# S5's tables in two buffer sets with their parameters on GpSimd, and MoBA's bias rows in 32 pieces

## The chip, the cores and the metric

The kernel runs on one core of one Trainium2 chip. The metric is the time of the slowest core in device microseconds (us); lower is better. The engines are TensorE (PE in the profile), VectorE (DVE), ScalarE (ACT), GpSimd (POOL) and SyncE (SP), which here only issues DMAs. Each engine works through its own instructions strictly in the order in which the program was built, and waits on semaphores for the others.

## What is computed

A stack of four layers on 256 tokens of width 1024 in float32. A layer is an FFN, a mixer and an FFN again, each behind an RMS norm and added to the residual. The mixers are S5, HGRN2, a gated delta net and MoBA attention, in this order. The change touches the first FFN (beside which S5's parameters are prepared), S5, and the FFN behind S5 (beside which MoBA's rows of relative-position bias are written).

```python
def _swiglu(x, w_gate, w_up, w_down):
    return (jax.nn.silu(x @ w_gate) * (x @ w_up)) @ w_down

...

def _s5_mixer(u, lam_re, lam_im, log_dt, b_re, b_im, c_re, c_im, d_skip, w_glu):
    f32 = jnp.float32
    bsz, L, _ = u.shape
    lam = lax.complex(jnp.minimum(lam_re.astype(f32), -1e-4), lam_im.astype(f32))
    dt = jnp.exp(log_dt.astype(f32))[:, None]
    lam_bar = jnp.exp(lam * dt)
    b_bar = ((lam_bar - 1.0) / lam)[..., None] * lax.complex(b_re.astype(f32), b_im.astype(f32))
    ug = u.astype(f32).reshape(bsz, L, S5_GROUPS, S5_GROUP)
    bu = jnp.einsum('blgh,gph->lbgp', ug, b_bar)
    a = jnp.broadcast_to(lam_bar, (L, 1) + lam_bar.shape)

    def combine(e1, e2):
        a1, b1 = e1
        a2, b2 = e2
        return a1 * a2, a2 * b1 + b2

    _, h = lax.associative_scan(combine, (a, bu), axis=0)
    c = lax.complex(c_re.astype(f32), c_im.astype(f32))
    y = jnp.einsum('lbgp,ghp->blgh', h, c).real.reshape(bsz, L, D_MODEL)
    y = y + d_skip.astype(f32) * u.astype(f32)
    y = jax.nn.gelu(y).astype(u.dtype)
    val, gate = jnp.split(y @ w_glu, 2, axis=-1)
    return val * jax.nn.sigmoid(gate)
```

MoBA adds `table_t[:, _t5_bucket(qpos - kpos)]`, a bias by head and distance, to its attention logits.

## The kernel before

**Weights and steps.** All weights stream from HBM by DMAs on SP's queue (L69) into four raw buffers. ScalarE casts each unit of 128x1024 to `hi` (L86), VectorE subtracts to get `lo` (L87), and TensorE multiplies with both in three products (L343 to L345). There are four `hi` and four `lo` buffers, so a unit is cast at most four units ahead of its use. One unit, 12 matmuls of 512 columns, is a *step* of an FFN; the first FFN has 66, 44 for gate and up and 22 for down. After every four gate and up steps a column pair j is done: L423 (ScalarE, silu) and L426 (VectorE, gate times up) run once for each half of the tokens, and two to four steps later TensorE transposes the result (L435) and L438, L439 split it.

**Work beside the first FFN.** `step()` calls the generator `s5_prep` once or not at all per step (before: on odd steps from 5 to 31, then on every step up to 59):

```python
                if self.prep is not None and n > 4:
                    for _ in range(n % 2 if n < 32 else 1 if n < 60 else 0):
                        next(self.prep, None)
```

`s5_prep` loads S5's parameters, transposes lambda (`lam_in`, L606) and b and c (L621) on TensorE, and computes exp (`exp_m1`), sin and cos (`sin_cos_m1`), the powers `pw` of the transition (by `cmul`), its phase brought to length one (`unit`), and the factor for b (L671 to L682), all on tiles of 128x64 (`s5small`). For eight blocks j it then builds the tables: GpSimd makes the inward half (L728 to L730, twice three instructions of 128x512), VectorE the outward half (L733, L734, L736, 128x1024), both in one tile `s5e`. TensorE forms the token kernel from it (L742) and transposes the inward half (L756); the tables go to DRAM (`s_out`, `s_k`, `s_in`). Last, `s5_phases` computes the powers of the phase for the scan on GpSimd, for the first half of the groups.

**S5.** `load` in `s5` fetches the tables back from DRAM into five buffers (`tab`; inward, token and outward ones, each in four parts). The second half of the phases is computed on GpSimd once the FFN is done. `xr` (L939) and the half-turn `tb` (L894, beside VectorE's scan at L900) run on GpSimd as well; `busy` (L249) fills TensorE's time with matmuls without use.

**MoBA's bias rows.** `moba_bias` runs in the FFN behind S5: it spreads a table over 8 rows of 384 on GpSimd and writes `bias_rows` (8 x 128 x 384, 1536 KB) to DRAM with one DMA on ScalarE's queue (L1713).

**What sets the order.** The program is written in the order of the calls; a scheduler of the framework then moves instructions within each engine's order by what they depend on, except those that `keep_in_program_order` pins. Buffers come from pools: a tile with the tag of an earlier one waits until that one's last reader is done.

## Time and profile before

| what | us |
|---|---|
| median of 3 runs (2221.56 to 2225.37) | 2224.2 |
| the profiled execution | 2227.23 |
| its span | 2225.5 |
| first FFN, TensorE's first to last matmul | 9.9 to 243.7 |
| S5, up to its gated output's first matmul | 243.7 to 296.1 |
| GpSimd, table blocks j = 0 to 7 | 109.6 to 204.3 |
| GpSimd, phases, first half | 205.6 to 230.2 |
| bias rows, issue of the write | 348.7 |

The page of a profile gives busy times per engine and per group of instructions; a line number is that of the kernel. The window view gives the same for stretches of the span, with the granted TensorE clock (1.00 is full speed). The wait view names what an engine waited for last: `PE aux L756 <- POOL s5e L730` is TensorE at L756 waiting for GpSimd's write of `s5e` at L730. `SPq` and `ACTq` rows are the issues of DMAs on these queues; their duration is that of the issue, not of the transfer.

### The profile page before, as it was taken

How to read it: one execution, taken by the hardware profiler on the slowest of the kernel's cores; microseconds unless marked ns; L12 is line 12 of the kernel's file. 1: busy time of each engine (PE TensorE's matmuls, PEld its weight loads, DVE VectorE, ACT ScalarE, POOL GpSimd, SP SyncE). 2: the span in 40 equal slices, each digit the busy share in tenths (PEclk: the TensorE clock that was granted, in tenths of full speed). 3: DMA queues.
4: the chain of work that ended last, by engine and by line, in shares of the span. 5: the costliest groups of instructions: out<-in, count | busy, mean ns of one | idle time of the engine just before them, and what ended most of it. 6: DMA issues, size and time to landing. Idle time of an engine off the chain costs nothing.

```text
span 2225.5 us, 30259 instructions
## 1 busy us (share of the span) xinstructions
PE 2142.0 (96%) x11480; PEld 1768.3 (79%) x11480; DVE 1452.5 (65%) x2445; ACT 1159.0 (52%) x1876; POOL 207.8 (9%) x272
## 2 busy tenths in 40 slices
PE   8988888999999999999999999998999999999998
PEld 6766666888888888888788887787888888898886
DVE  7987674556555977555655788887555555666555
ACT  6434344445444855444544677764544544555443
POOL 0598600000000000001000000000000000000000
PEclk9999999999999999999999999999999999999999
DMA  8655966655555554655555543334555655655553
GB/s 252 191 193 200 250 184 161 205 175 191 186 189 190 171 168 136 189 178 189 176 180 176 163 141 105 105 115 131 175 186 180 199 182 187 199 162 170 189 180 105
DMA packets 317907, 389.64 MB, mean 175 GB/s; under 512 B 14192, under 2 KB 247856, under 8 KB 316736
## 3 DMA queue, kind: packets, MB, share of 16 engines
q1 hardware_dynamic: 314768, 383.92, 54.5%
q10 hardware_dynamic: 2800, 3.68, 0.9%
q8 instruction: 90, 1.47, 0.3%
q14 instruction: 57, 0.47, 0.1%
q0 software_dynamic: 192, 0.10, 0.0%
HBM read 375.65 MB, written 12.01 MB: 174 GB/s over the span
## 4 chain that ended last, share of the span: by engine, by line
PE 80%; ACT 5%; DVE 5%; issue 4%; DMA 3%; POOL 2%; SPq 0%; ACTq 0%; POOLq 0%; DVEq 0%
PE acc L343 23%; PE acc L345 23%; PE acc L344 23%; PE acc L311 2%; PE aux L435 2%; PE acc L312 2%; DVE lo L87 2%; PE acc L313 2%; ACT hi L86 1%; DMA raw<-in_ffn_w_up_dram 1%; ACT zb L1512 1%; PE aux L226 1%; POOL s5e L730 1%; POOL s5e L729 1%; POOL s5tmp L728 1%
## 5 line engine op out<-in xcount | busy, mean ns | idle before, releaser
L87 DVE TENSOR_TENSOR lo<-raw,hi 128x1024 fp32r<-128x1024 f32 x681 | 850.0, 1250 | 585.3 <-ACT hi L86 583.6
L86 ACT CAST hi<-raw 128x1024 fp32r<-128x1024 f32 x681 | 713.0, 1049 | 703.0 <-PE acc L345 648.0
L343 PE MATMUL acc<-hi,xhl 128*128 128x512 f32 x1568 | 625.7, 399 | 8.6 <-ACT hi L86 8.2
L344 PE MATMUL acc<-lo,xhl 128*128 128x512 f32 x1568 | 615.9, 393 | 2.4 <-DVE lo L87 2.3
L345 PE MATMUL acc<-hi,xhl 128*128 128x512 f32 x1568 | 615.3, 393 | 0.0
L343 PEld LDWEIGHTS acc<-hi,xhl 128*128 128x128 f32 x1568 | 296.1, 189 | 70.8 <-ACT hi L86 9.1
L345 PEld LDWEIGHTS acc<-hi,xhl 128*128 128x128 f32 x1568 | 296.0, 189 | 64.4 <-issue 0.9
L344 PEld LDWEIGHTS acc<-lo,xhl 128*128 128x128 f32 x1568 | 296.6, 189 | 63.6 <-DVE lo L87 5.1
L343 PE MATMUL acc<-hi,hhl 128*128 128x512 f32 x704 | 276.3, 392 | 0.0
L345 PE MATMUL acc<-hi,hhl 128*128 128x512 f32 x704 | 276.1, 392 | 0.0
L344 PE MATMUL acc<-lo,hhl 128*128 128x512 f32 x704 | 275.0, 391 | 0.0
L344 PEld LDWEIGHTS acc<-lo,hhl 128*128 128x128 f32 x704 | 132.5, 188 | 27.4
L345 PEld LDWEIGHTS acc<-hi,hhl 128*128 128x128 f32 x704 | 132.5, 188 | 27.4
L343 PEld LDWEIGHTS acc<-hi,hhl 128*128 128x128 f32 x704 | 132.6, 188 | 27.0
L313 PE MATMUL acc<-xhl,lo 128*128 128x256 f32 x520 | 150.0, 290 | 0.0
L311 PE MATMUL acc<-xhl,hi 128*128 128x256 f32 x520 | 149.7, 291 | 0.0
L312 PE MATMUL acc<-xhl,hi 128*128 128x256 f32 x520 | 148.4, 288 | 0.0
L423 ACT ACTIVATE sl<-acc,norm_r 128x256 f32<-128x256 f32 x176 | 83.6, 475 | 109.3 <-PE acc L345 88.6
L426 DVE TENSOR_TENSOR h<-acc,sl 128x256 f32<-128x256 f32 x176 | 74.0, 420 | 49.8 <-ACT sl L423 49.8
L313 PEld LDWEIGHTS acc<-xhl,lo 128*128 128x128 f32 x520 | 100.1, 193 | 2.0 <-DVE lo L87 1.0
L311 PEld LDWEIGHTS acc<-xhl,hi 128*128 128x128 f32 x520 | 99.7, 193 | 1.8 <-issue 0.9
L312 PEld LDWEIGHTS acc<-xhl,hi 128*128 128x128 f32 x520 | 99.9, 193 | 1.3 <-issue 1.1
(563 smaller groups left out, 2148.5 us busy)
## 6 DMA issues: line engine op xcount, KB each, us to landing
raw<-in_ffn_w_gate_dram SPq DMA_DIRECT2D x174, 512.0 KB, 3.8
raw<-in_ffn_w_up_dram SPq DMA_DIRECT2D x174, 512.0 KB, 4.8
raw<-in_ffn_w_down_dram SPq DMA_DIRECT2D x80, 1024.0 KB, 4.9
raw<-in_gdn_w_in_dram SPq DMA_DIRECT2D x24, 1024.0 KB, 5.2
raw<-in_hg_w_in_dram SPq DMA_DIRECT2D x16, 1024.0 KB, 5.4
raw<-in_moba_w_in_dram SPq DMA_DIRECT2D x12, 1024.0 KB, 5.1
raw<-in_ffn_w_down_dram SPq DMA_DIRECT2D x16, 512.0 KB, 3.7
raw<-in_s_w_glu_dram SPq DMA_DIRECT2D x16, 512.0 KB, 6.1
```

Of the source, the lines that this page charges most:

```text
L86: pin(self.nc.scalar.copy(hi, src))
L87: self.nc.vector.tensor_tensor(lo, src, hi.bitcast(F32), op=OP.subtract)
L226: nc.tensor.transpose(q[:, j * 128:j * 128 + 128], self.x[:, t, k * 128:k * 128 + 128], self.ident)
L311: t.matmul(p, hi, ah, start=first, stop=False)
L312: t.matmul(p, hi, al, start=False, stop=False)
L313: t.matmul(p, lo, ah, start=False, stop=last)
L343: mm(p, ah, hi[:, j], start=first and j == 0, stop=False)
L344: mm(p, ah, lo[:, j], start=False, stop=False)
L345: mm(p, al, hi[:, j], start=False, stop=last and j == n - 1)
L423: nc.scalar.activation(sl, p[:, :256], AF.Silu, scale=self.r_col[:, t:t + 1])
L426: return nc.vector.tensor_tensor(waiting[-1][1][:, t], p[:, 256:], sl, op=OP.mult)
L435: nc.tensor.transpose(q[:, c:c + 128], h[:, t, f * 128:f * 128 + 128], self.ident)
```

## The change

- `exp_m1`, `sin_cos_m1`, the powers and the phase unit run on GpSimd in place of VectorE. [...] The copies of the unit into `s5l` and of `pw` into `s5kk` go from GpSimd to ScalarE (L680 and L724 of the new kernel). The factor for b stays on VectorE (L686 to L697).
- The tables get a second set, `s5f` beside `s5e`; blocks j alternate. A block takes four calls of `s5_prep` in place of two, and its inward half is transposed one block later (`turned(j - 1)`). `step()` calls the generator at step 2, 6 to 18, and from 26 on.
- `s5_load` is taken out of `s5`, there are six `tab` buffers in place of five, and the first six loads (four inward, two token parts) are written in `s5_prep`, with one phase step behind each.
- The bias rows are written by 32 DMAs of 48 KB, one per step of the FFN.

```diff
             steps = [0]
+            bias = None
+            if self.prep is None and self.bias is not None:
+                bias = self.bias(pool)
+                self.bias = None
 
             def step():
                 steps[0] += 1
                 n = steps[0]
                 if n % 4 == 1 and waiting and n > 4:
                     turn()
-                if self.prep is not None and n > 4:
-                    for _ in range(n % 2 if n < 32 else 1 if n < 60 else 0):
-                        next(self.prep, None)
+                if bias is not None and n > 4:
+                    next(bias, None)
+
+                if self.prep is not None and (n == 2 or 5 < n < 19 or n > 25):
+                    next(self.prep, None)
...
+    def stt(self, eng, out, a, s, b, op0, op1, t=None):
+
+        t = out if t is None else t
+        eng.tensor_scalar(t, a, s, None, op0=op0)
+        eng.tensor_tensor(out, t, b, op=op1)
+
     def exp_m1(self, slots, x):
 
-        v = self.nc.vector
+        v = self.nc.gpsimd
...
-        v.scalar_tensor_tensor(r, n, -0.693359375, r, op0=OP.mult, op1=OP.add)
-        v.scalar_tensor_tensor(r, n, 2.12194440e-4, r, op0=OP.mult, op1=OP.add)
+        self.stt(v, r, n, -0.693359375, r, OP.mult, OP.add, t)
+        self.stt(v, r, n, 2.12194440e-4, r, OP.mult, OP.add, t)
...
+        g = nc.gpsimd
         _, dt = yield from self.exp_m1(slots, dt_in)
         yield
         ab = [slots.pop(), slots.pop()]
         for out, a in zip(ab, (lr, li)):
-            v.tensor_tensor(out, a, dt, op=OP.mult)
+            g.tensor_tensor(out, a, dt, op=OP.mult)
...
-        v.scalar_tensor_tensor(nr, cm, 1.0, em, op0=OP.add, op1=OP.mult)
-        v.tensor_tensor(nr, nr, cm, op=OP.add)
-        v.tensor_tensor(ni, ex, sn, op=OP.mult)
-        v.memset(pw[:, 0, :, 0], 1.0)
-        v.memset(pw[:, 1, :, 0], 0.0)
-        v.tensor_scalar(pw[:, 0, :, 1], nr, 1.0, None, op0=OP.add)
-        v.tensor_copy(pw[:, 1, :, 1], ni)
+        self.stt(g, nr, cm, 1.0, em, OP.add, OP.mult)
...
-                      [tmp[:, c, :64 * m].rearrange("p (g m) -> p g m", m=m) for c in range(2)])
+                      [tmp[:, c, :64 * m].rearrange("p (g m) -> p g m", m=m) for c in range(2)], g)
...
-        self.unit((cs, sn8), (tmp[:, 0, :64], tmp[:, 0, 64:128]), v)
+            g.tensor_tensor(tmp[:, 0, :64], cs, cs, op=OP.mult)
+            g.tensor_tensor(tmp[:, 0, 64:128], sn8, sn8, op=OP.mult)
+            self.stt(g, sn8, cs, 2.0, sn8, OP.mult, OP.mult, tmp[:, 0, 128:192])
+            g.tensor_tensor(cs, tmp[:, 0, :64], tmp[:, 0, 64:128], op=OP.subtract)
+            g.tensor_tensor(ex, ex, ex, op=OP.mult)
+        self.unit((cs, sn8), (tmp[:, 0, :64], tmp[:, 0, 64:128]), g)
         self.s5_l = pool.tile([128, 3, 32], F32, name="s5l")
-        for q in range(4):
+
+        def places(q):
             for a in range(2):
                 for n, t in enumerate((cs, sn8, ex)):
-                    nc.gpsimd.tensor_copy(self.s5_l[q * 32:q * 32 + 32, n].rearrange("p (j g a) -> p j g a", j=8, g=2)[:, :, :, a],
-                                          t[a * 32:a * 32 + 32].rearrange("p (j q g) -> p j q g", j=8, q=4)[:, :, q])
+                    nc.scalar.copy(self.s5_l[q * 32:q * 32 + 32, n].rearrange("p (j g a) -> p j g a", j=8, g=2)[:, :, :, a],
+                                   t[a * 32:a * 32 + 32].rearrange("p (j q g) -> p j q g", j=8, q=4)[:, :, q])
+
+        yield
...
+        places(0)
         yield
...
+        places(1)
...
+        places(2)
+        places(3)
...
-            nc.gpsimd.tensor_copy(back[:, :, :, n], pw[:, :, :, 8 - n])
+            nc.scalar.copy(back[:, :, :, n], pw[:, :, :, 8 - n])
         e = pool.tile([128, 16, 128], F32, name="s5e", tag="s5C")
-        eo, ebs = e[:, :8], (e[:, 8:12], e[:, 12:16])
+        more = pool.tile([128, 16, 128], F32, name="s5f", tag="s5G")
+        eos = e[:, :8], more[:, :8]
+        ebs = [(t[:, 8:12], t[:, 12:16]) for t in (e, more)]
...
+        def turned(j):
+
+            for n, eb in enumerate(ebs[j % 2]):
+                p = self.aux.tile([128, 512], F32, name="aux")
+                for g in range(4):
+                    nc.tensor.transpose(p[:, g * 128:g * 128 + 128], eb[:, g], self.ident)
+                nc.scalar.copy(et.rearrange("p g c -> p (g c)"), p)
+                dma(as_ap(self.s5_in, (8 * j + 4 * n) * 128, [[8192, 128], [128, 4], [1, 128]]), et)
+
         for j in range(8):
             r = slice(8 * j, 8 * j + 8)
-
-            rs = (slice(8 * j, 8 * j + 4), slice(8 * j + 4, 8 * j + 8))
-            for h, eb in zip(rs, ebs):
+            eo = eos[j % 2]
+
+            for n, eb in enumerate(ebs[j % 2]):
+                h = slice(8 * j + 4 * n, 8 * j + 4 * n + 4)
...
             dma(as_ap(self.s5_out, j * 1024, [[8192, 128], [128, 8], [1, 128]]), eo)
+            yield
...
+            if j:
+                turned(j - 1)
             yield
-            for h, eb in zip(rs, ebs):
-                p = self.aux.tile([128, 512], F32, name="aux")
-                for g in range(4):
-                    nc.tensor.transpose(p[:, g * 128:g * 128 + 128], eb[:, g], self.ident)
-                nc.scalar.copy(et.rearrange("p g c -> p (g c)"), p)
-                dma(as_ap(self.s5_in, h.start * 128, [[8192, 128], [128, 4], [1, 128]]), et)
-
+            yield
+        turned(7)
+
+        self.s5_tags = ["s5" + c for c in "ABCDEG"]
+        self.s5_tabs = []
         self.s5_turn = pool.tile([128, 2, 16, 32], F32, name="s5turn", tag="s5pw")
-        yield from self.s5_phases(self.s5_turn, 0, pool)
+        phases = self.s5_phases(self.s5_turn, 0, pool)
+        for kind, part in (("in", 0), ("in", 1), ("in", 2), ("in", 3), ("t", 0), ("t", 1)):
+            self.s5_tabs.append(self.s5_load(kind, part))
+            next(phases, None)
+            yield
...
+    def s5_load(self, kind, part):
+
+        tags = self.s5_tags
+        tags.append(tags.pop(0))
+        t = self.s5_pool.tile([128, 16, 128], F32, name="tab", tag=tags[-1])
+        if kind == "t":
+
+            for s in range(8):
+                self.nc.sync.dma_start(t[s * 16:s * 16 + 16],
+                                       as_ap(self.s5_k, part * 16 * 3840 + (7 - s) * 16, [[240, 16], [3840, 16], [1, 128]]))
+        else:
+            src = self.s5_in if kind == "in" else self.s5_out
+            self.nc.sync.dma_start(t, as_ap(src, part * 2048, [[8192, 128], [128, 16], [1, 128]]))
+        return t.rearrange("p (j q g) c -> p j q g c", q=4, g=2)
...
-        tags = ["s5" + c for c in "ABCDE"]
+        tags = self.s5_tags
...
+            if self.s5_tabs:
+                return self.s5_tabs.pop(0)
+            return self.s5_load(kind, part)
...
-        nc.scalar.dma_start(self.bias_rows, row.rearrange("h (o s) -> h o s", o=1).to_broadcast([8, 128, 384]))
+        for k in range(0, 128, 4):
+            yield
+            self.tc.keep_in_program_order(nc.scalar.dma_start(
+                as_ap(self.bias_rows, k * 384, [[128 * 384, 8], [384, 4], [1, 384]]),
+                row.rearrange("h (o s) -> h o s", o=1).to_broadcast([8, 4, 384])))
```

What the change moves on VectorE, in the first FFN around the second column pair (L87 is a weight's `lo`, L426 gate times up, L439 the split). Before, the rows from the tenth L87 on:

```order
L87 TENSOR_TENSOR lo<-raw,hi 128x1024 x2
L426 TENSOR_TENSOR h<-acc,sl 128x256 x2
L87 TENSOR_TENSOR lo<-raw,hi 128x1024
L607 TENSOR_SCALAR s5small<-aux 128x64
L608 COPY s5small<-aux 128x64
```

The changed kernel, from the eleventh L87 on:

```order
L87 TENSOR_TENSOR lo<-raw,hi 128x1024
L426 TENSOR_TENSOR h<-acc,sl 128x256
L691 TENSOR_TENSOR s5small<-s5small 128x64
L426 TENSOR_TENSOR h<-acc,sl 128x256
L690 TENSOR_TENSOR s5small<-s5small 128x64
L692 TENSOR_TENSOR s5small<-s5small 128x64
L695 TENSOR_TENSOR s5small<-s5small 128x64
```

L691 and L690 multiply with the transition minus one, which GpSimd now makes (L655 and L654), and they stand around the second L426 of the pair.

On ScalarE of the changed kernel, the rows from the thirteenth cast on (L680 copies the unit, L423 is the silu, L438 the split's cast); before, no copy of this kind stood on ScalarE:

```order
L86 CAST hi<-raw 128x1024 x2
L680 COPY s5l<-s5small 32x16 x3
L86 CAST hi<-raw 128x1024
L680 COPY s5l<-s5small 32x16 x4
L423 ACTIVATE sl<-acc,norm_r 128x256
L680 COPY s5l<-s5small 32x16 x9
L86 CAST hi<-raw 128x1024
L423 ACTIVATE sl<-acc,norm_r 128x256
L680 COPY s5l<-s5small 32x16 x8
```

The copies, which need the end of GpSimd's unit, now stand ahead of cast 15 and of the third pair's L423.

On SP's queue at the end of the first FFN (`s_in`, `s_out` and `s_k` are the tables in DRAM, `tab` their buffers for S5, `w_glu` S5's output weights), before:

```order
L758 DMA s_in<-s5tmp 128x512
L69 DMA raw<-in_ffn_w_down_dram 128x2x512
L69 DMA raw<-in_s_w_glu_dram 128x4x256 x2
L804 DMA tab<-s_in 128x2048
L69 DMA raw<-in_s_w_glu_dram 128x4x256 x2
L804 DMA tab<-s_in 128x2048
L69 DMA raw<-in_s_w_glu_dram 128x4x256 x4
L804 DMA tab<-s_in 128x2048 x2
L800 DMA tab<-s_k 16x16x128 x16
L804 DMA tab<-s_out 128x2048 x2
```

and in the changed kernel:

```order
L748 DMA s_in<-s5tmp 128x512
L829 DMA tab<-s_in 128x2048
L748 DMA s_in<-s5tmp 128x512
L69 DMA raw<-in_s_w_glu_dram 128x4x256 x2
L748 DMA s_in<-s5tmp 128x512
L69 DMA raw<-in_s_w_glu_dram 128x4x256 x2
L829 DMA tab<-s_in 128x2048 x3
L825 DMA tab<-s_k 16x16x128 x13
L829 DMA tab<-s_out 128x2048 x2
```

The last writes of the inward table now lie between the loads of S5's output weights, and three inward tables and 13 pieces of the token tables behind them; three pieces stand earlier, between the last weights of the FFN.

More of the change, by code (lines that the diff above doesn't have):

```diff
@@ L455, in ffn @@
             nc.vector.tensor_scalar(half, self.r_col, 0.5, None, op0=OP.mult)
-            if self.prep is None and self.bias is not None:
-                self.bias(pool)
-                self.bias = None
             ahead = self.ahead
@@ L540, in sin_cos_m1 @@
     def sin_cos_m1(self, slots, x):
-        v = self.nc.vector
-        t, n, r, z, s, c, a, b, k, odd = [slots.pop() for _ in range(10)]
-        k, odd = k.bitcast(I32), odd.bitcast(I32)
+        v = self.nc.gpsimd
+        t, n, r, z, s, c, a, b = [slots.pop() for _ in range(8)]
         big = 12582912.0
```

58 lines of the change are left out of this document (25 added, 33 removed).

## The prediction

> **What bounds the kernel now.** The page comes first: the busy time of each engine over the whole span.
>
> ```profile
> PE 2142.0 (96%) x11480; PEld 1768.3 (79%) x11480; DVE 1452.5 (65%) x2445; ACT 1159.0 (52%) x1876; POOL 207.8 (9%) x272
> ```
>
> TensorE is busy for 96% of the span, so an edit off TensorE can only win where TensorE stands still or runs at a lowered clock. The change touches the first FFN (to about 244 us), S5 behind it (to about 296) and the FFN after that. Second, the windows over the stretches in question (columns: from:to, us, busy time and instructions of PE, PEld, DVE, ACT and POOL, the granted PE clock, DMA share, GB/s):
>
> ```profile
> 10.00:100.00 90.00, 87.39 (x396) 69.57 (x397) 82.69 (x225) 54.04 (x81) 19.09 (x26) 1.00 0.71 218
> 100.00:240.00 140.00, 122.53 (x664) 97.10 (x663) 104.22 (x78) 57.98 (x89) 117.37 (x109) 0.96 0.64 218
> 140.00:150.00 10.00, 5.22 (x21) 3.90 (x20) 9.90 (x7) 2.84 (x5) 9.76 (x6) 0.70 0.56 198
> 370.00:390.00 20.00, 12.70 (x45) 9.58 (x44) 5.08 (x7) 5.30 (x7) 0.00 (x0) 0.74 0.79 210
> ```
>
> Up to 100 us TensorE loses 2.6 of 90 us: **there it is the bound, and what is put in its way costs in full**. From 100 to 240 it is idle for 17.5 us, and the clock of 0.96 costs 4% of 122.5, 4.9 more: 22.4 us are to be won. The row of 140 to 150 shows what a stall leaves behind: 5.22 busy us at 0.70 lose another 1.6. Around 380 us stands a third loss.
>
> Third, TensorE's waits up to 330 us, by what ended them (total, times, longest):
>
> ```profile
> PE acc L878 <- DMA tab<-s_k: 11.9, 3, 5.0
> PE aux L756 <- POOL s5e L730: 11.2, 5, 3.5
> PE aux L742 <- DVE s5e L736: 6.2, 3, 3.2
> ```
>
> L756 and L742 work on S5's tables within the first FFN, and POOL and DVE deliver these too late; L878 is S5 itself.
>
> **The change part by part. GpSimd's chain.** exp, sin and cos, the powers and the phase unit leave DVE for GpSimd. DVE's pace in that chain, and GpSimd's with the same shape in the phases, from the timeline (start, us):
>
> ```profile
> 47.15 0.22 DVE L526 TENSOR_TENSOR s5small<-s5small 128x64 f32<-128x64 f32 x1
> 47.41 0.20 DVE L527 TENSOR_SCALAR s5small<-s5small 128x64 f32<-128x64 f32 x1
> 47.64 0.23 DVE L528 TENSOR_TENSOR s5small<-s5small 128x64 f32<-128x64 f32 x1
> ```
>
> ```profile
> 212.47 0.31 POOL L495 TENSOR_TENSOR s5t<-s5turn 128x64 f32<-128x64 f32 x1
> 212.74 0.31 POOL L496 TENSOR_TENSOR s5t<-s5turn 128x64 f32<-128x64 f32 x1
> 213.13 0.32 POOL L497 TENSOR_TENSOR s5turn<-s5t 128x64 f32<-128x64 f32 x1
> 213.53 1.20 POOL L498 TENSOR_TENSOR s5t<-s5turn 128x64 f32<-128x64 f32 x1
> ```
>
> DVE does two dependent instructions in 0.49 us, 0.245 each. On GpSimd an independent one follows after 0.27, a dependent one after 0.39, and one that meets a two-input DVE instruction takes 0.9 longer (1.20 for 0.31). One-input instructions of this shape are not in the trace. The ends are 0.27 (nothing depends) and 0.42 (all depend, some meet DVE); I take **0.35**, nearer the upper one, since most of the chain depends and half of it has one input.
>
> The Trainium skill ("GPSIMD Engine Reference", 4.1 Engine selection) calls GpSimd about two times slower than VectorE at two-input elementwise work and near line rate with one input. The rows give 0.31 to 0.22, or 1.4, at this size. By a factor of two the pitch would be 0.49, and the sum by it stands among the rivals.
>
> When does the chain start, and who waits for it? TensorE's and DVE's timelines around its start:
>
> ```profile
> 29.77 0.39 PE L343 MATMUL acc<-hi,xhl 128*128 128x512 f32 x1
> ...
> 32.95 0.39 PE L345 MATMUL acc<-hi,xhl 128*128 128x512 f32 x1
> ...
> 39.36 0.27 PE L606 MATMUL aux<-ident,lam_in 64*128 64x64 f32 x1
> ...
> 41.39 1.10 PE L621 MATMUL aux<-ident,s5b_in 64*128 64x64 f32 x8
> 42.42 0.66 PE L435 MATMUL aux<-ident,h 128*128 128x128 f32 x4
> ```
>
> ```profile
> 37.03 0.42 DVE L426 TENSOR_TENSOR h<-acc,sl 128x256 f32<-128x256 f32 x1 [0.94 <-ACT sl L423]
> 37.97 1.23 DVE L87 TENSOR_TENSOR lo<-raw,hi 128x1024 fp32r<-128x1024 f32 x1 [0.51 <-ACT hi L86]
> ```
>
> Places in TensorE's order are told in weight steps of 12 matmuls; from 29.77 to 32.95 the first and last of 15 stand, so one takes 0.227 and a step 2.73. Lambda's second transpose (39.36, step 9.08) moves to step 6.75, which is 39.36 - 2.33 x 2.73 = 33.0, and its copy ends at about 33.4. Then, in GpSimd's new order, 71 instructions end with L655: at 0.35 that is 58.3, with a meeting or so **59**. Up to the end of the powers stand 11 small ones and 18 of 64 to 256 columns (0.36, 0.5 and 0.7 each, between the row of 64 and one of 512 below): **74** with a few meetings. The unit has 21 small ones (7.4), the 1024-column L703 stands among them (about 2), and meetings with DVE add some 3: **86**. So the chain is 52.6 us long, and 0.01 of pitch moves its end by 1.5.
>
> In DVE's new order L691, which reads L655's product, stands ahead of the second L426 of the column pair j = 1. That one ran at 37.03; now it runs at 59.5, and TensorE's transposes L435 wait for it at step 9.08. Undisturbed, TensorE would be there at 43 (39.4 and some 3.6 for the 32 transposes L632 that now stand ahead, at most 1.10 per eight). It starts at 60.5: **17 us** of waiting. Since weights are cast at most four steps ahead, nothing runs meanwhile. At about 86 the second wait ends: ScalarE's copies L680, which stand behind its cast 14 and read the unit. GpSimd's time for these is known:
>
> ```profile
> L667 POOL COPY s5l<-s5small 32x16 f32<-32x16 f32 x24 | 14.6, 609 | 66.1 <-DVE s5small L661 55.8 <-DVE s5small L510 9.4
> ```
>
> On ScalarE the trace has none; between 0 and 0.61 each I take 0.25. Sixteen of them stand ahead of the second L423 of j = 2, 4 us, and with two casts, L423 and L426 the product comes at 94.5. TensorE's transposes at step 13.08, due at 43 + 4 x 2.73 + 0.6 = 54.4, start at 94.8: **+40.4**, and with two restarts at 1.6 **+43.6**. A pitch of 0.27 makes it 32, 0.42 makes it 54.
>
> **Steps 31 to 61.** Two table sets, and four steps per j in place of two, take the waits of L742 and L756 away: **-22.4**. What is late next? GpSimd and DVE slow each other. First the two groups from 109.6 to 204.3 us (busy, mean ns), then each of the two operations in a moment with less company (the L87 at 37.97 above is alone):
>
> ```profile
> L730 POOL TENSOR_TENSOR s5e<-s5e,s5tmp 128x512 f32<-128x512 f32 x16 | 31.6, 1975 | 0.6
> ```
>
> ```profile
> L87 DVE TENSOR_TENSOR lo<-raw,hi 128x1024 fp32r<-128x1024 f32 x22 | 40.5, 1842 | 14.3 <-ACT hi L86 14.3
> ```
>
> ```profile
> 109.62 1.06 POOL L728 TENSOR_TENSOR s5tmp<-s5D,s5kk 128x512 f32<-128x512 f32 x1
> ```
>
> 1.06 becomes 1.98, and 1.23 becomes 1.84. In 94.7 us eight tables and 22 L87 were done: 11.8 us per j with 2.75 of them. With four it is 11.8 + 1.25 x 1.23 = 13.4. TensorE needs 4 x 2.73 and twelve transposes of 0.165 in four steps of gate and up, some 13.0, and with eight of them 12.2 in four of down. Of j = 2 to 7 most stand in the down part, and **+5** is left over: net **-17.4**.
>
> The Trainium skill ("SBUF — State Buffer", Who interferes with whom) has a two-input VectorE instruction and a GpSimd instruction that reads SBUF shut each other out for a whole instruction. The trace agrees nearly: by it a j of before is (2.75 + 2.5) x 1.23 + 6 x 1.06 = 12.8, and 11.8 was measured. By the rule a new j takes 15.0, which would leave 14 us in place of 5.
>
> **S5.** What ends it now, by the chain of waits; SP's issues of the table pieces; DVE's longest wait there; GpSimd's phases, first half 205.61 to 230.16, second from 243.99:
>
> ```profile
> 260.72 12.02 DMA tab<-s_out
> 272.75 6.30 DMA tab<-s_k
> ```
>
> ```profile
> 237.70 22.11 SPq L800 DMA_DIRECT2D tab<-s_k  x16
> ```
>
> ```profile
> DVE inc L900 <- POOL tb L894: 7.2, 1, 7.2
> ```
>
> ```profile
> 205.61 0.22 POOL L495 TENSOR_TENSOR s5t<-s5turn 128x16 f32<-128x16 f32 x1
> ...
> 229.73 0.43 POOL L500 TENSOR_TENSOR s5turn<-s5t 128x112 f32<-128x112 f32 x1
> 243.99 0.13 POOL L768 MEMSET turn<- 128x16 f32 x1 [13.83 <-PE acc L345]
> ```
>
> Six tables are asked for within the FFN, but on SP three inward ones and 13 of 16 pieces of the token tables stand behind the last write of the inward table, whose copy on ScalarE follows cast 66, so about 1 us ahead of the FFN's end. Then come the landing of that write, the three tables and 13 pieces at 1.38 (22.11 / 16), 18 us: done 20 us or so behind the FFN's end, where before it was 16 (259.8 against 244): **+3 on SP**. GpSimd gets later too: its last table waits for TensorE's step 55.25, some 33 us ahead of the end; 13.4 for the table and 24.5 for the first half end 5 us behind the FFN's end, and the second half, which started right at that end, starts 5 later. DVE waits for it already. The two lie beside each other, and with the little slack that GpSimd has I take **+4**; the ends are -4 (SP meets free buffers and shorter issues) and +6.
>
> **The bias rows.** TensorE's wait from 370 to 390 us, and the issues on ScalarE's and SP's queues ahead of it:
>
> ```profile
> PE acc L343 <- ACT hi L86: 6.8, 1, 6.8
> ```
>
> ```profile
> 348.66 0.79 ACTq L1713 DMA_DIRECT2D bias_rows<-row  x1
> ```
>
> ```profile
> 364.80 9.74 SPq L69 DMA_DIRECT2D raw<-in_ffn_w_up_dram  x1
> ```
>
> Behind one write of 1536 KB an issue of weights took 9.74 us, and TensorE ran 45 matmuls in 20 us where 88 fit. If 48 KB a step leave no hole, 43 x 0.227 = **-9.8**. The 32 issues at 0.79 are 25 us of ScalarE, hidden in its idle time (busy 54 of 90 us in the first FFN); without that cover one delays a cast by 0.8. The ends are 0 and -9.8; I take the gain.
>
> **Sum.** 43.6 - 17.4 + 4 - 9.8 = **+20.4** on the profiled execution's 2227.2 us (a span of 2225.5 and 1.7 around it): 2247.6. The median of the runs lies 3.0 lower, at 2224.2, so the forecast is **2244.6**.
>
> **Rivals.**
> - *GpSimd's small operations are quick* (the other side: faster). One-input instructions could need far less than 0.27, and the early wait shrinks by 1.5 per 0.01. This decides below a pitch of 0.21, where the sum is nothing; at 0.15 it is 20.4 - 30 = -9.6, or 2214.6. Without any early wait it would be 2201. Against it: 16 columns (205.61) still take 0.22.
> - *GpSimd at twice DVE's time*: a pitch of 0.49, +21, 2266. For it stands that all the chain depends; against it the 0.39 at 212.74.
> - *Full exclusion in steps 31 to 61*: +9, 2254. The 11.8 against 12.8 speaks against it.
> - *The bias pieces win nothing*, since all 1536 KB are still written: +9.8, 2254. Against it: 48 KB in 2.73 us are 18 GB/s beside some 210.
>
> **How the numbers follow.** The forecast gets 0.57 (2232 to 2256, by pitches of 0.27 to 0.42 and S5's ends), quick operations 0.16, twice DVE's time 0.07, full exclusion 0.10, the bias 0.10. The range leaves out the quicker half of the first rival and the slowest of the others: 2210 to 2264. A measurement of this kernel tells about 0.2%, 4.4 us, from no change. Faster by more than that: 0.16, the first rival. Within it: 0.09, the forecast's low end. Slower: 0.75.
>
> **What would show it.** Right: DVE's L691 and ScalarE's L680 wait for POOL; TensorE's waits name L435 <- DVE with some 17 us, and about 20 more before 100 us; L774 and L746, the new lines of L742's and L756's work, wait for under 6 us together; the FFN behind S5 has no wait for a cast; GpSimd's second half of the phases starts 5 us behind S5's start. Wrong: TensorE passes step 13.08 before 75 us, or the chain has a pitch under 0.25; then the sign of the sum turns.

## The result, and the profile after

The changed kernel takes **2248.1 us**, the median of 4 runs (2245.5 to 2252.1); before took 2224.8 in 4 runs on the same chip (2221.6 to 2225.9). The ratio is 1.011, with a 95% interval of 1.0097 to 1.0123: slower by about 1.1%. The forecast was 2244.6 in a range of 2210 to 2264.

The two profiled executions lie 19.0 us apart (spans of 2244.5 and 2225.5), the medians 23.4: the profiled one of before lies 2.4 above its median, that of after 1.9 below. So sums over the traces explain 19, and some 4 us are scatter between executions.

The page of after, busy time of each engine:

```profile
PE 2137.8 (95%) x11480; PEld 1766.9 (79%) x11480; DVE 1439.5 (64%) x2311; ACT 1166.5 (52%) x1908; POOL 253.4 (11%) x390
```

GpSimd has 46 us more work, DVE 13 less; TensorE's work is the same, and its share of a longer span is lower. Where it stands still is shown by the windows of after (columns as before: from:to, us, busy time of PE, PEld, DVE, ACT and POOL, clock, DMA share, GB/s):

```profile
10.00:100.00 90.00, 56.71 (x224) 43.13 (x225) 42.53 (x69) 42.67 (x90) 70.24 (x152) 0.77 0.46 142
100.00:240.00 140.00, 125.22 (x644) 100.03 (x643) 112.28 (x85) 58.32 (x79) 80.42 (x42) 0.98 0.58 191
...
50.00:60.00 10.00, 0.00 (x0) 0.00 (x0) 0.00 (x0) 0.00 (x0) 9.28 (x32) 0.50 0.00 0
```

Up to 100 us TensorE is busy for 56.71 us at a mean clock of 0.77, where before it was for 87.39 at 1.00 (the 0.77 is a mean over the idle stretches too, so it can't be multiplied with the busy time). **The loss lies there: the third column pair already comes 37.4 us later (the table below), more than the whole difference.** From 50 to 60 us one engine alone works, and no byte moves: everything waits for GpSimd's chain.

The same is told by the waits up to 350 us (total, times, longest), first TensorE's, then DVE's, then ScalarE's:

```profile
PE aux L435 <- DVE h L426: 42.7, 9, 17.0
PE aux L993 <- DVE sc L990: 6.1, 2, 4.7
...
PE acc L920 <- DMA tab<-s_k: 4.0, 2, 3.6
```

```profile
DVE s5small L691 <- POOL s5small L655: 18.2, 1, 18.2
...
DVE s5e L765 <- POOL s5pw L503: 7.2, 1, 7.2
```

```profile
ACT s5l L680 <- POOL s5small L513: 16.1, 1, 16.1
```

L742 and L756 of before (6.2 and 11.2 us for the tables, together 17.4) are now L774 and L746, and no longer appear among the waits, as was meant. L435, the transposes of gate times up, have come in their place; L920 and L993 are S5. DVE waits for L655 and ScalarE for the end of the unit (L513), each once and long.

For the accounting the start of the program is cut at five places that both traces have: the third and the seventh column pair of the first FFN (start of the pair's last row of L435), the end of that FFN (TensorE's first fillers behind it), the end of S5 (the first matmul of its output weights; in before it is at 293.7, and the 296.1 given ahead of the prediction is where these matmuls go on behind a wait), and the last L345 on `xhl` ahead of 720 us.

| us of the trace | 3rd pair | 7th pair | FFN end | S5 end | last L345 |
|---|---|---|---|---|---|
| before | 55.6 | 102.5 | 243.7 | 293.7 | 664.9 |
| after | 93.0 | 148.3 | 279.7 | 328.5 | 689.0 |
| stretch up to here in after, less that in before | +37.4 | +8.4 | -9.8 | -1.2 | -10.7 |

### The profile page after: what moved, and what is told of

It is laid out like the page before. It is cut to its first block, busy times and chain, and to the rows that moved or that the text cites. A ratio compares the mean times of both kernels' runs of the same rounds, so it can differ in the third digit from the quotient of the medians.

```text
span 2244.5 us, 30317 instructions
## 1 busy us (share of the span) xinstructions
PE 2137.8 (95%) x11480; PEld 1766.9 (79%) x11480; DVE 1439.5 (64%) x2311; ACT 1166.5 (52%) x1908; POOL 253.4 (11%) x390
## 4 chain that ended last, share of the span: by engine, by line
PE 79%; DVE 6%; ACT 5%; issue 5%; POOL 4%; DMA 1%; SPq 0%; ACTq 0%; POOLq 0%; DVEq 0%
PE acc L343 23%; PE acc L344 23%; PE acc L345 23%; DVE lo L87 2%; PE aux L435 2%; PE acc L311 2%; PE acc L312 2%; PE acc L313 2%; ACT hi L86 1%; ACT zb L1554 1%; PE aux L226 1%; DMA s_in<-s5tmp 0%; POOL xr L981 0%; DVE s5tmp L764 0%; DVE s5f L767 0%
## 5 line engine op out<-in xcount | busy, mean ns | idle before, releaser
L87 DVE TENSOR_TENSOR lo<-raw,hi 128x1024 fp32r<-128x1024 f32 x681 | 852.2, 1254 | 551.6 <-ACT hi L86 547.1
L345 PE MATMUL acc<-hi,xhl 128*128 128x512 f32 x1568 | 617.0, 394 | 0.0
L345 PEld LDWEIGHTS acc<-hi,xhl 128*128 128x128 f32 x1568 | 296.9, 189 | 63.8 <-issue 0.9
L345 PE MATMUL acc<-hi,hhl 128*128 128x512 f32 x704 | 275.6, 392 | 0.0
L345 PEld LDWEIGHTS acc<-hi,hhl 128*128 128x128 f32 x704 | 132.2, 188 | 27.5
L423 ACT ACTIVATE sl<-acc,norm_r 128x256 f32<-128x256 f32 x176 | 83.5, 475 | 98.2 <-PE acc L345 82.5
L426 DVE TENSOR_TENSOR h<-acc,sl 128x256 f32<-128x256 f32 x176 | 73.9, 420 | 70.9 <-ACT sl L423 70.9
```

What stands on the lines that cost most here:

```text
L87: self.nc.vector.tensor_tensor(lo, src, hi.bitcast(F32), op=OP.subtract)
L345: mm(p, al, hi[:, j], start=False, stop=last and j == n - 1)
L423: nc.scalar.activation(sl, p[:, :256], AF.Silu, scale=self.r_col[:, t:t + 1])
L426: return nc.vector.tensor_tensor(waiting[-1][1][:, t], p[:, 256:], sl, op=OP.mult)
```

## The experiments

Ten kernels, each timed in runs that alternate with the kernel before on the same chip; "pinned" means `keep_in_program_order`, which holds an instruction at the place where the code issues it, in place of one that the scheduler chooses. Differences below are each kernel's median against before on its own chip; the changed kernel's is +23.4. The ratio isn't formed from these two medians and can differ from them by some 0.001, or 2 us. Stretches of a kernel are read from one traced execution each: the first FFN of bias_alone has the instructions of before in the same order on each engine, and ends at 246.8 where before's ends at 243.7. So a stretch that differs by some 3 us shows nothing.

| kernel | median us | before, same chip | difference | ratio, 95% interval |
|---|---|---|---|---|
| chain_dve | 2221.6 | 2222.6 | -1.0 | 0.9992 (0.9982 to 1.0002) |
| bias_alone | 2213.9 | 2222.6 | -8.7 | 0.9955 (0.9937 to 0.9973) |
| tables_alone | 2224.6 | 2224.3 | +0.4 | 1.0003 (0.9992 to 1.0014) |
| pin_users | 2225.3 | 2222.6 | +2.7 | 1.0005 (0.9994 to 1.0017) |
| pin_unit_users | 2245.0 | 2223.8 | +21.2 | 1.0095 (1.0073 to 1.0116) |
| half_inward | 2240.9 | 2222.6 | +18.3 | 1.0077 (1.0062 to 1.0092) |
| pin_tables | 2245.9 | 2224.3 | +21.7 | 1.0098 (1.0075 to 1.0121) |
| pin_both | 2220.5 | 2224.3 | -3.8 | 0.9985 (0.9973 to 0.9997) |
| tables_bias | 2213.3 | 2223.8 | -10.5 | 0.9951 (0.9936 to 0.9966) |
| tables_place | 2207.6 | 2223.8 | -16.2 | 0.9932 (0.9916 to 0.9947) |

### Which part costs, and which gains

**chain_dve**: the change with its whole chain back on VectorE, still as unfused instructions (`stt` issues two for each fused one of before).

```diff
     def exp_m1(self, slots, x):
 
-        v = self.nc.gpsimd
+        v = self.nc.vector
...
     def sin_cos_m1(self, slots, x):
 
-        v = self.nc.gpsimd
+        v = self.nc.vector
...
-        g = nc.gpsimd
+        g = nc.vector
```

> The changed kernel with the chain (exp, sin, cos, powers, unit) back on VectorE, in the same unfused instructions; copies, tables, loads and bias rows as in the changed kernel. Theory A: no wait for GpSimd before 100 us, VectorE is fuller by about 120 instructions of 0.1 to 0.25 us (some 20 us spread over 60), TensorE loses under 6 us of the first 100, and the time is 2204 to 2214. Theory B would give the same here, so this run measures what the move itself cost: 34 to 44 us by Theory A and the forecast's term of 43.6. If the time is above 2235, the early loss does not come from the move at all.

From +23.4 to -1.0: **moving the chain to GpSimd, with the order that the scheduler makes of it, costs 24.4 us**. The third pair comes at 56.0 us, as before. That is less than the 34 to 44 expected, because this kernel is slower than expected itself (2204 to 2214): its first FFN ends at 253.3, 9.6 behind before, and TensorE waits there for VectorE's gate products:

```profile
PE aux L435 <- DVE h L426: 20.6, 10, 5.3
```

**bias_alone**: before, with the bias rows in 32 pieces, one per step.

```diff
...
-        nc.scalar.dma_start(self.bias_rows, row.rearrange("h (o s) -> h o s", o=1).to_broadcast([8, 128, 384]))
+        for k in range(0, 128, 4):
+            yield
+            self.tc.keep_in_program_order(nc.scalar.dma_start(
+                as_ap(self.bias_rows, k * 384, [[128 * 384, 8], [384, 4], [1, 384]]),
+                row.rearrange("h (o s) -> h o s", o=1).to_broadcast([8, 4, 384])))
```

> The kernel before with the bias rows in 32 pieces and nothing else. Forecast's term: -9.8, the wait for a cast at about 376 us gone: 2214 to 2216 (0.995 to 0.996). Rival (1536 KB are written all the same, or 32 issues delay casts): 2222 to 2226, with waits for casts left in that FFN.

A gain of 8.7 us. TensorE's wait for a cast in this FFN is gone. The window of bias_alone for the 20 us in which before ran 45 matmuls at a clock of 0.74:

```profile
370.00:390.00 20.00, 20.00 (x94) 16.48 (x93) 10.62 (x12) 9.35 (x12) 0.00 (x0) 1.00 0.57 176
```

In the trace of after, the bias tile's own view gives the issues (shortest, median and longest in ns, first and last start):

```profile
L1757 ACTq DMA_DIRECT2D bias_rows<-row x32: 270/285/346, 391.6 to 487.8; - x32
```

32 issues of 0.285 are 9 us of ScalarE, spread over 96, not the 25 that one issue's 0.79 had suggested.

**tables_alone**: before, with the two table sets, four calls a block, the new call steps and the six early loads; the chain stays fused on VectorE, the copies on GpSimd, the bias in one DMA.

```diff
-                if self.prep is not None and n > 4:
-                    for _ in range(n % 2 if n < 32 else 1 if n < 60 else 0):
-                        next(self.prep, None)
+                if self.prep is not None and (n == 2 or 5 < n < 19 or n > 25):
+                    next(self.prep, None)
...
-        eo, ebs = e[:, :8], (e[:, 8:12], e[:, 12:16])
+        more = pool.tile([128, 16, 128], F32, name="s5f", tag="s5G")
+        eos = e[:, :8], more[:, :8]
+        ebs = [(t[:, 8:12], t[:, 12:16]) for t in (e, more)]
```

> The kernel before with the tables' part alone: two sets, four calls per block, transposes one block later, steps 26 and later, six loads written in the first FFN; chain fused on VectorE, copies on GpSimd, one bias DMA, as before. The forecast's terms are -17.4 and +4, so 2209. The runs so far speak otherwise: chain_dve lies 7.7 above bias_alone, so by them the tables' part costs 4 to 10 us, 2226 to 2232, with waits of TensorE for L426 in place of those for the tables, and a first FFN that ends 5 to 10 us later than before's 243.7 to 246.8.

No change within its interval; by the forecast's terms it would have been 2209, and 2226 to 2232 was expected from the runs ahead of it. Its first FFN ends at 242.6, S5 takes 52.8 us in place of 50.0. TensorE's longest wait in it, by its total:

```profile
PE aux L435 <- DVE h L426: 15.6, 9, 3.1
```

The waits for the tables have gone, and 15.6 us of short waits for L426 stand there without any chain on GpSimd. So the tables' part wins nothing by itself, without any chain on GpSimd.

So the +23.4 are made of: the bias -8.7; the tables +0.4; the chain unfused, with its copies on ScalarE, +7.3 (what chain_dve's -1.0 leaves beside these two; against tables_bias below, which has both in one kernel, it is +9.5); and the chain's engine +24.4.

### The early waits

**pin_users**: the change, with the readers of the chain's results pinned: VectorE's factor for b, the 1024-column products, ScalarE's copies, and the table products of the first two blocks.

```diff
-        v.tensor_tensor(fi, ni, li, op=OP.mult)
+        pin(v.tensor_tensor(fi, ni, li, op=OP.mult))
...
-                    nc.scalar.copy(
+                    pin(nc.scalar.copy(
...
+            hold = (lambda ins: ins) if j > 1 else pin
+            hold(v.tensor_tensor(ta, c1[:, r].unsqueeze(2).to_broadcast(w), pp[0], op=OP.mult))
```

> The changed kernel with one thing more: the instructions of VectorE and ScalarE that read GpSimd's chain (the factor for b, the copies of the unit and of the powers, the first two blocks' outward products) are kept at the place of their call, step 26 and later, and so no longer stand ahead of the second L426 of the second column pair; GpSimd's chain is unchanged. Theory A (the order: the chain is slow, but costs only because readers of it stand in front of work that TensorE needs): the 42.7 us of TensorE waiting for L426 fall below 12, the first FFN ends near 240 us, and the time is 2205 to 2213 (0.992 to 0.996 of the kernel before). Theory B (GpSimd's chain slows VectorE and TensorE by its length wherever it is waited for): the wait only moves to step 26, and the time stays above 2235. The meetings of GpSimd with L87 make the chain longer here, as VectorE no longer stands still: its end is expected near 100 us, not 87.

The third pair is back at 54.8 us: **with the chain still on GpSimd, order alone takes its wait away**. But from +23.4 to +2.7 the time falls by 20.7, not by the early wait's 37 to 46. The rest comes back later: 2205 to 2213 was expected with an FFN that ends near 240 and waits for L426 under 12 us, and the FFN ends at 255.7 and these waits are 20.4. ScalarE's timeline at the unit's end, and the window in which the delayed readers and the tables meet:

```profile
97.14 1.02 ACT L681 COPY s5l<-s5small 32x16 f32<-32x16 f32 x6 [6.38 <-POOL s5small L513]
```

```profile
100.00:170.00 70.00, 47.99 (x235) 37.12 (x234) 69.59 (x53) 29.21 (x56) 59.83 (x28) 0.84 0.49 161
```

The unit ends at 97.4 in place of 86.8, with VectorE at work beside the chain. From 100 to 170 us VectorE is busy for 69.59 of 70 us and TensorE for 47.99: VectorE is the bound.

**pin_unit_users**: only the readers of the unit pinned: ScalarE's copies and the three 1024-column products. It asks whether the loss is one wait or two.

```diff
-                    nc.scalar.copy(
+                    pin(nc.scalar.copy(
...
-            eng.tensor_tensor(t, b, fw[1], op=OP.mult)
+            pin(eng.tensor_tensor(t, b, fw[1], op=OP.mult))
```

> The changed kernel with only the second group of readers kept at the place of their call: ScalarE's copies of the unit and the powers, and the three 1024-wide products of VectorE, which write a buffer that GpSimd's unit still uses. L691 and the hoisted outward product L765 (which waits for the powers, done at 74 us) stay in front. By the forecast's decomposition the first wait stays at 17 us (L691 near 60), and the second ends with the powers instead of the unit: the third pair's L435 comes at 82 to 85 us in place of 93.0. The rival, one wait only (L691 alone sets the delay, what follows is catching up): it stays at 91 to 94. The total says less, since the readers meet the tables' work later, as in pin_users: 2228 to 2242.

Two. VectorE's timeline has the third pair's gate products behind the wait for the powers (which stays):

```profile
79.11 0.41 DVE L426 TENSOR_TENSOR h<-acc,sl 128x256 f32<-128x256 f32 x1
...
81.88 0.41 DVE L426 TENSOR_TENSOR h<-acc,sl 128x256 f32<-128x256 f32 x1
```

TensorE goes on at 82.4 in place of 93.0, and at the seventh pair it leads the changed kernel by 20.7 us (127.6 against 148.3). At the FFN's end 3.2 us are left (276.5). The pinned products run from 122 to 131 us, where the first blocks already need them, and from 127 to 170 us VectorE has no idle stretch, while most of its instructions of 1024 columns take 1.5 to 2.3 us beside GpSimd. Three of its rows:

```profile
134.72 2.07 DVE L768 TENSOR_TENSOR s5e<-s5e,s5tmp 128x1024 f32<-128x1024 f32 x1
136.72 2.07 DVE L87 TENSOR_TENSOR lo<-raw,hi 128x1024 fp32r<-128x1024 f32 x1
138.72 2.07 DVE L765 TENSOR_TENSOR s5tmp<-s5E,s5pw 128x1024 f32<-128x1024 f32 x1
```

The second wait was taken away and its loss moved: the difference is +21.2, and 2245.0 lies above the 2228 to 2242 expected.

### Steps 31 to 61

Here the forecast had throughput in mind: VectorE and GpSimd slow each other, by 5 us in all, or by 14 if they shut each other out entirely. The trace of after suggests another cause, the order on VectorE.

**half_inward** takes half of GpSimd's work in a block away: the second half of the inward table isn't computed, and zeros stand in its place.

```diff
+        for eb in ebs:
+            nc.gpsimd.memset(eb[1], 0.0)
...
-            for n, eb in enumerate(ebs[j % 2]):
+            for n, eb in enumerate(ebs[j % 2][:1]):
```

> The changed kernel without the second of the two inward halves of each block (24 of GpSimd's 48 instructions L759 to L761 are left out, a constant stands in that half). Theory C (in steps 31 to 61 GpSimd and VectorE exclude each other, so a block takes longer than TensorE's four steps): TensorE's losses between 160 and 250 us, some 12 us, fall below 3, and the time is 8 to 14 us under the changed kernel's. Theory D (the losses come from the place of the tables in VectorE's order, not from GpSimd's company): they stay above 8, and the time is within 4 us of the changed kernel's. The early wait is the same in both.

From the seventh to the eleventh pair it takes 62.1 us, the changed kernel 62.8. **Half of GpSimd's products less, and these four pairs are no quicker**: neither GpSimd's throughput nor the exclusion sets their period. (TensorE's idle time from 160 to 250 us is 6.6 us for 11.0, between what the two theories expected.) The gain (+18.3 for +23.4) lies ahead of the seventh pair: from the third, at 93.0 in both, it takes 50.0 us there in place of 55.3. So where the first blocks meet the delayed chain, GpSimd's company does cost some 5 us.

**pin_tables** keeps all of GpSimd's work and pins VectorE's three table products where the code issues them.

```diff
-            v.tensor_tensor(ta, c1[:, r].unsqueeze(2).to_broadcast(w), pp[0], op=OP.mult)
-            v.tensor_tensor(split(eo), c2[:, r].unsqueeze(2).to_broadcast(w), pp[1], op=OP.mult)
+            pin(v.tensor_tensor(ta, c1[:, r].unsqueeze(2).to_broadcast(w), pp[0], op=OP.mult))
+            pin(v.tensor_tensor(split(eo), c2[:, r].unsqueeze(2).to_broadcast(w), pp[1], op=OP.mult))
             yield
-            v.tensor_tensor(split(eo), split(eo), ta, op=OP.add)
+            pin(v.tensor_tensor(split(eo), split(eo), ta, op=OP.add))
```

> The changed kernel with VectorE's outward products (three per block) kept at the place of their call, so that none stands between the two L426 of a column pair; the chain's readers stay where the changed kernel has them (early wait as there). Between the transposes L435 of pairs 6 and 10 (148.3 and 211.1 us) the changed kernel takes 62.8 us, and half_inward, with half of GpSimd's table work left out, 62.1: so GpSimd's share is not what sets that pace. Theory D (the place: L767 and L764 stand ahead of the L426 that TensorE's L435 needs one step later): the stretch falls below 56 and the time is 5 to 10 us under the changed kernel's, 2238 to 2243. Theory C (throughput of GpSimd and VectorE together): the stretch stays above 60 and the time within 3 us of 2248.

The same four pairs take 56.2 us, 6.6 less: the order was at work there. But from the eleventh pair to the end of the FFN it takes 75.2 where the changed kernel takes 68.6, so from the seventh pair on nothing is won (131.4 for 131.5); the FFN ends 4.8 earlier, at 274.9, because the seventh pair comes that much earlier (143.5). The time hardly falls (+21.7; 2238 to 2243 was expected), and TensorE's waits say where the gain went:

```profile
PE aux L435 <- DVE h L426: 26.8, 5, 17.0
PE acc L921 <- DMA tab<-s_k: 14.6, 4, 6.1
...
PE aux L775 <- DVE s5f L768: 5.1, 3, 2.4
```

L435 waits 15.9 less, but L775 (the token kernel, L774 of the changed kernel) now waits for VectorE's last product of a block, and S5 waits 10.6 more for its token tables and takes 55.6 us in place of 48.8. On SP's queue 15 of their pieces stand behind the end of the FFN in place of 13, and they are out at 297.8 us, for 298.0 in the changed kernel: the loads didn't come earlier with the FFN.

### What can be had of the change

**pin_both**: pin_users and pin_tables together, with the unit ahead of the powers.

```diff
-        for n, m in ((1, 1), (2, 2), (4, 4)):
-            self.cmul([pw[:, c, :, n + 1:n + m + 1] for c in range(2)], [pw[:, c, :, 1:m + 1] for c in range(2)],
...
         self.unit((cs, sn8), (tmp[:, 0, :64], tmp[:, 0, 64:128]), g)
+        yield
+        for n, m in ((1, 1), (2, 2), (4, 4)):
+            self.cmul([pw[:, c, :, n + 1:n + m + 1] for c in range(2)], [pw[:, c, :, 1:m + 1] for c in range(2)],
...
```

> pin_users and pin_tables together, with GpSimd's unit computed ahead of the powers, so that the copies of the unit find it done (in pin_users ScalarE waited 6.4 us for it at 97 us). If the three losses add up: the first FFN of 255.7 us in pin_users falls by some 6 for the wait and 5 to 10 for the place, to 240 to 246, and the time is 2206 to 2214, under the kernel before by 0.4 to 0.7%. If GpSimd's and VectorE's throughput is the bound (Theory C), it stays at 2218 to 2225.

-3.8: with every reader in a place of its own the third pair stands at 55.1 and the chain on GpSimd costs no more than in chain_dve (the intervals overlap). But -8.7 of it are the bias rows', so the rest is still a loss. S5 waits 15.3 us for its token tables, and in the first FFN (which ends at 248.5) the token kernel waits for VectorE's last product:

```profile
PE aux L775 <- DVE s5e L768: 6.3, 3, 3.8
PE aux L775 <- DVE s5f L768: 6.1, 4, 2.4
```

The losses didn't add up to the 2206 to 2214 expected: 2220.5 lies in the range given to the other theory, the throughput of GpSimd and VectorE together. Whether that or the new places make L775 wait was not separated.

**tables_bias** is tables_alone with the bias pieces of bias_alone, and has no edit of its own.

> tables_alone and bias_alone together: the changed kernel with its chain as before on VectorE (fused) and the copies on GpSimd. If the parts add up: 2224.6 - 8.7 = 2216, within 3. By the forecast's own terms for these parts (-17.4, +4, -9.8) it would be 2199 to 2202.

-10.5, near the sum of its parts (+0.4 and -8.7).

**tables_place**: tables_bias with pin_tables' edit, and the blocks from step 23 on, so that the tables are early enough for S5.

```diff
-                if self.prep is not None and (n == 2 or 5 < n < 19 or n > 25):
+                if self.prep is not None and (n == 2 or 5 < n < 19 or n > 22):
```

> tables_bias with VectorE's outward products kept at the place of their call and the blocks called three steps earlier (from step 23 on). If the tables' part gained nothing because L426 stands behind the outward products and because the tables are late for S5, both are mended here: waits for L426 under 4 us, the first FFN ends 4 to 9 us under tables_alone's 242.6, S5 takes 50 to 52 us, and the time is 2204 to 2211, the fastest of all. If GpSimd and VectorE are the bound together, other waits (for the tables, L742's and L756's work) take the place again and the time stays at 2213 to 2218.

**2207.6 us, 0.9932 of before (0.9916 to 0.9947), the lowest of all.** TensorE's waits, and three rows of VectorE's timeline:

```profile
PE acc L906 <- DMA tab<-s_k: 14.0, 3, 5.9
PE aux L760 <- DVE s5f L753: 5.2, 3, 2.2
...
PE aux L760 <- DVE s5e L753: 4.0, 2, 2.6
...
PE aux L435 <- DVE h L426: 2.1, 3, 1.2
```

```profile
162.20 1.21 DVE L753 TENSOR_TENSOR s5e<-s5e,s5tmp 128x1024 f32<-128x1024 f32 x1
163.34 1.21 DVE L87 TENSOR_TENSOR lo<-raw,hi 128x1024 fp32r<-128x1024 f32 x1
164.47 0.41 DVE L426 TENSOR_TENSOR h<-acc,sl 128x256 f32<-128x256 f32 x1
```

VectorE's last table product (L753) now runs ahead of the L426 at its quick 1.21, L435 waits 2.1 us in place of 15.8 in tables_bias, and the first FFN ends at 238.9, 4.8 ahead of before and 3.7 ahead of tables_alone (4 to 9 expected). In its place the token kernel (L760) waits 9.2 us for L753, so VectorE is still late for TensorE. Its interval overlaps with that of tables_bias, so the 5.7 us between these two medians are likely rather than settled. S5 still waits 14.0 for token tables.

## Why the prediction was right, and where it was not

The sign and the size were right, and the early wait that makes them came by the mechanism that was named. Two of four terms were off, in opposite directions, and 5 us came from where nothing was forecast, so that the sum came out within 1.4 us is partly luck. In us of the profiled executions:

| term | forecast | measured | from |
|---|---|---|---|
| early wait | +43.6 | +45.8 | start of the 7th pair, 102.5 to 148.3 |
| steps 31 to 61 | -17.4 | -9.8 | 7th pair to FFN end, 141.2 to 131.5 |
| S5 | +4 | -1.2 | FFN end to S5's end, 50.0 to 48.8 |
| bias rows | -9.8 | -10.7 | S5's end to the cut ahead of 720 us, 371.2 to 360.5 |
| the rest | 0 | -5.1 | from there to the end |
| sum | +20.4 | +19.0 | spans |

**The early wait** came as told up to the third pair. GpSimd's timeline of after: the first of the 71 instructions, L655 as the last, the end of the powers and the end of the unit:

```profile
33.59 0.33 POOL L644 TENSOR_TENSOR s5small<-s5small 128x64 f32<-128x64 f32 x1 [2.69 <-DVE s5small L619]
...
59.74 0.32 POOL L655 TENSOR_TENSOR s5small<-s5small 128x64 f32<-128x64 f32 x1
...
73.52 0.72 POOL L503 TENSOR_TENSOR s5pw<-s5tmp 128x256 f32<-128x256 f32 x1
...
86.20 0.59 POOL L513 TENSOR_TENSOR s5small<-s5small,s5tmp 128x64 f32<-128x64 f32 x2
```

That is 33.6, 60.1, 74.2 and 86.8 where 33.4, 59, 74 and 86 were forecast; the pitch is 26.5 / 71 = 0.373, for 0.35. VectorE's timeline shows the wait and who stood behind it:

```profile
41.46 0.42 DVE L426 TENSOR_TENSOR h<-acc,sl 128x256 f32<-128x256 f32 x1 [5.01 <-ACT sl L423]
60.09 0.33 DVE L691 TENSOR_TENSOR s5small<-s5small 128x64 f32<-128x64 f32 x1 [18.21 <-POOL s5small L655]
60.34 0.41 DVE L426 TENSOR_TENSOR h<-acc,sl 128x256 f32<-128x256 f32 x1
```

One small product that needs GpSimd's result stands between the two L426 of a pair, and the second L426 starts 23 us later than before. The third pair's L426 came at 92.5 (94.5 forecast) and L435 at 93.0 (94.8). The two rivals on the pitch, under 0.21 and 0.49, are out.

The second wait shows less on L435 than the "about 20 more": TensorE waits 4.5 us for an L87 behind the wait for the powers, then 7.2 and 3.7 for L426. And the +45.8 is near +43.6 by two misses. At the third pair the delay is 37.4, for 40.4 (it came at 55.6 before, where 54.4 was assumed). Then 8.4 us follow up to the seventh pair, for two restarts of 1.6: VectorE runs the delayed products and the first blocks' there, TensorE waits 5.6 for L426, and half_inward does without some 5 of it.

The 0.373 is the pitch beside a VectorE that mostly waits. In pin_users, where VectorE works on, the same product ends at 69.6, and (69.6 - 33.7) / 71 = 0.51. So 0.35 came near with a VectorE that stood still; beside a working one the pitch is that of the rival. The forecast counted on "a meeting or so" without saying why there would be so few, and that was luck.

**Steps 31 to 61 is the step that failed.** The forecast took all of the 22.4 us as won but for "+5 is left over", and that 5, from "With four it is 11.8 + 1.25 x 1.23 = 13.4", counted work against work. What showed instead is that L435 waits for L426 where the tables were waited for. Of -17.4 the changed kernel has -9.8, and even that flatters the term, as the first blocks' products run ahead of the seventh pair there: tables_alone, which has no early wait, ends the FFN only 1.1 us ahead of before, and its waits for L426 are 15.6 us. In the changed kernel the blocks come every 16 to 18 us (the last L435 of the pairs at 160.5, 177.2, 193.5 and 211.1), though VectorE and GpSimd wait in each of them. VectorE's timeline over one block, and GpSimd's first row in it:

```profile
183.62 1.22 DVE L765 TENSOR_TENSOR s5e<-s5E,s5pw 128x1024 f32<-128x1024 f32 x1 [1.01 <-PE aux L774]
184.76 2.08 DVE L87 TENSOR_TENSOR lo<-raw,hi 128x1024 fp32r<-128x1024 f32 x1
186.76 2.07 DVE L767 TENSOR_TENSOR s5e<-s5e,s5tmp 128x1024 f32<-128x1024 f32 x1
188.76 0.41 DVE L426 TENSOR_TENSOR h<-acc,sl 128x256 f32<-128x256 f32 x1
189.10 1.98 DVE L764 TENSOR_TENSOR s5tmp<-s5E,s5pw 128x1024 f32<-128x1024 f32 x1
191.00 2.07 DVE L87 TENSOR_TENSOR lo<-raw,hi 128x1024 fp32r<-128x1024 f32 x1
193.00 0.41 DVE L426 TENSOR_TENSOR h<-acc,sl 128x256 f32<-128x256 f32 x1
```

```profile
184.22 3.54 POOL L760 TENSOR_TENSOR s5f<-s5D,s5kk 128x512 f32<-128x512 f32 x2 [4.31 <-PE aux L746]
```

and what waits for VectorE's last row, on TensorE:

```profile
193.46 0.90 PE L435 MATMUL aux<-ident,h 128*128 128x128 f32 x3 [3.06 <-DVE h L426]
```

TensorE's L774 and L746 free VectorE (183.62) and GpSimd (184.22) almost together, so from then on VectorE runs at 2.07; and the scheduler has set L767 and L764, 4 us of products that nobody needs yet, ahead of the two L426 for which TensorE waits 3.06. Late L435 mean a late L746, and for that GpSimd had waited 4.31 at the block's start. half_inward speaks against GpSimd's throughput, and pin_tables shows the order at work (62.8 to 56.2 us for four pairs). But pin_tables has lost that gain by the end of the FFN, and wherever VectorE's products are pinned the token kernel waits for the last of them. So the order makes the waits for L426, and what sets the length of the whole stretch, VectorE's work in it or its order, stays open. The rival of full exclusion had about the right total for this stretch (-22.4 + 14 = -8.4, against -9.8), but half_inward doesn't bear out its reason.

The Trainium skill ("SBUF — State Buffer", Who interferes with whom) has a two-input VectorE instruction and a GpSimd instruction that reads SBUF exclude each other. The 2.07 beside GpSimd and 1.22 alone agree with it; that halving GpSimd's work left the four pairs at 62.1 shows that the rule, though it holds for the instructions, did not set their time.

**S5** has two errors in it. GpSimd's last block was released by L746 at 247.0, 32.7 ahead of the FFN's end (33 forecast), and the five of the block's six instructions that were left took 6.7 us: the "13.4 for the table" is the period of a block, not GpSimd's work in it. So the first half of the phases was done at 277.1, and the second started 0.3 behind the FFN's end (279.7), not 5:

```profile
280.02 0.13 POOL L804 MEMSET turn<- 128x16 f32 x1 [2.89 <-ACT hi L86]
```

On SP the 13 token pieces are out at 298.0, 18.2 behind that end, and the wait for them is 4.0 in place of 11.9. Yet S5 is only 1.2 shorter, because the phases and VectorE's scans behind them take as long as ever. VectorE's last transposes of the state, in before and in after:

```profile
288.03 1.31 DVE L948 STREAM_TRANSPOSE sc<-S 128x512 f32<-128x512 f32 x2
```

```profile
324.47 1.30 DVE L990 STREAM_TRANSPOSE sc<-S 128x512 f32<-128x512 f32 x2
```

That is 44.3 and 44.8 us behind the end of the FFN; what TensorE no longer waits for the tables it waits for these (L993, 6.1). The earlier loads had this wait next to them; and a difference of 1.2 us is less than the traces differ by.

**The bias rows** gained what was forecast (-10.7 in the traces, -8.7 alone by the medians), and the rival that they win nothing is out. The 5.1 us of **the rest** stay open: no edit touches it, and since single executions of one kernel differ by as much (2217.4 to 2229.8 in 19 runs of before), it may be scatter; no run was made to tell.

## What to carry to other kernels

Work moved to a slower, idle engine is paid for by its readers: before moving it, find where the scheduler will put each reader on the busy engines' in-order queues, since one small reader set too early there holds everything behind it for the whole length of the chain. Give such readers a place by hand, and then check that this place isn't where the engine is already full, and that what they feed isn't late for the next stage. And when a period is longer than the work in it, look at the order ahead of the instruction that the bound engine waits for, and follow what a fix gains to the end of the stage: here six of its microseconds were lost again there.

## What the runs showed of the hardware

On GpSimd an operation with one input isn't quicker than one with two at this size, unless it has two constants (or is a cast, 0.24). Three rows of the exponential in GpSimd's timeline of after: L533 has one input and two constants (multiply and add), L535 two inputs, L536 one input and one constant (add):

```profile
38.35 0.24 POOL L533 TENSOR_SCALAR s5small<-s5small 128x64 f32<-128x64 f32 x1
...
43.65 0.32 POOL L535 TENSOR_TENSOR s5small<-s5small 128x64 f32<-128x64 f32 x1
44.05 0.37 POOL L536 TENSOR_SCALAR s5small<-s5small 128x64 f32<-128x64 f32 x1
```

Two constants take 0.24, two inputs 0.32, one constant 0.37. It is so all over the chain (0.24 for every multiply and add with two constants, 0.37 to 0.39 for every one with a single constant, where no VectorE instruction was met); why isn't shown. Each starts some 0.08 behind the end of the one that it needs (43.65 + 0.32 to 44.05). The Trainium skill ("GPSIMD Engine Reference", 4.1 Engine selection) gives about two times VectorE's time for two inputs and roughly line rate for one; here the mixed, dependent chain took 0.373 against VectorE's 0.245 an instruction, 1.5 times. Small copies on ScalarE (32 by 16) took 0.17 each (1.02 for six, the row of pin_users), and while TensorE stood still its granted clock was 0.50 (50 to 60 us).
